# A fourth pair of weight parts, in borrowed homes, for two stretches of an fp32 up projection on one Trainium2 core

## The chip, the core and the metric

The kernel is one program on one core of one Trainium2 chip. The metric is the device time of one execution in microseconds (us). Shorter is better. The engines are named as the profile names them: PE (TensorE, matmuls), PEld (its weight loads), DVE (VectorE), ACT (ScalarE), POOL (GpSimd) and SP (SyncE, which issues most DMAs).

## The reference, cut to what matters

One layer of a decoder trunk, 256 tokens wide 2048, in float32: an RMSNorm, two token mixers, an output projection with a residual, and then the part that the change touches:

```
h = rmsnorm(x, norm_ffn_w)                       # 256 x 2048
gate, up = split(h @ w_up, 2)                    # w_up: 2048 x 11264, so 256 x 5632 each
gate = causal_dwconv(gate, conv_ffn_w) + conv_ffn_b
x = x + (gelu(gate) * up) @ w_down
return rmsnorm(x, norm_final_w)
```

## The kernel before, in words

**High and low parts.** PE multiplies a rounded format (`F32R`) here. To keep float32 accuracy, each operand is cut in two: a high part (the value cast to `F32R`) and a low part (value minus high). A product is then three matmuls: high by high, low by high, high by low. For each weight tile, ACT makes the high part `whi` (the cast, L289), and DVE makes the low part `wlo` (the split, L297: `raw - hi`). A tile is 128 x 2 x 512 (512 KB): 256 rows of the weight matrix by 512 columns.

**Rings.** The raw tile comes by an SP DMA (L209) into a ring of four buffers (tag `raw`). `whi` and `wlo` have rings of three buffers each (`wpool`, L62). `begin(n)` (L277) makes raw loads, casts and splits up to tile number n. `weights()` (L197) is called once for each tile, just ahead of its matmuls, and calls `begin(taken + AHEAD + 1)` with `AHEAD = 2`: when tile number t is used, tiles up to t+2 have been written into the program.

**The up projection.** Its 11264 columns are done in 11 chunks: chunk c covers 512 gate columns and 512 up columns. The 2048 rows are eight pairs of 128, `kp` 0 to 7. A *plain* tile (one column side, one `kp`) takes 12 matmuls (`up_plain`, L1412, through `high_first`, L1368). For chunks in `TWO` (1 to 7 and 9), rows 0 to 1023 are done in another way: in two groups of 512 rows (`ch` 1 first, then 0), a 2 by 2 block product by seven *part* products instead of eight block products (`up_product`, L1377). The blocks of the weights are b11 (first 256 rows of the group, gate), b12 (the same rows, up), b21 and b22 (the next 256 rows). They are loaded whole by SP into the `quad` tiles (`quad_load`, L218), and DVE makes four differences of them in place (`up_sum`, L225, instruction at L230), which with b11, b21 and b22 are the seven factors: T1, 11, T2, 21, T3, 22, T4. Each part tile is cast and split like a raw one, and takes 6 matmuls. Chunks 8 and 10 have one such group, chunk 0 none.

**Order of a step.** `up_steps` (L100 to L127) sets the order of PE by hand (L1446). From chunk 1 to the parts of chunk 7 the same cycle of 22 tiles repeats. I write b for group 1, a for group 0, g4 to g7 and u4 to u7 for the plain tiles of `kp` 4 to 7 on the gate and the up side. The cycle is

```
g4 g5 g6 g7 u4 | T1b u5 11b u6 T1a 11a u7 T2b T2a 21b 21a (turn gate) T3b T3a 22b 22a (turn up) T4b T4a
```

"Step k" below means the parts of chunk k together with the plain tiles of chunk k-1 that come ahead of them. The turns are eight transposes each (L1436) of the finished gate and up results of the chunk before. Beside the splits and the differences, DVE has in each step: two sums that carry a partial result from one PSUM bank to another (L1396 after T2a, which T3b's bank must wait for, since it reads bank `(0, 1)` that T3b goes on to write; and L1410 after T3a, the same with T4b), eight products of the causal convolution (`gate_part`, L1331, two for each of four slices, each pair behind an ACT instruction at L1326), two products of `up_part` (L1344) and the split of the finished result (L1352). These belong to the chunk before and are written into the program one piece at a time behind plain tiles (L1474).

**Who sets the order.** PE's order is that of the program text. The orders of DVE, ACT and of SP's DMA queue are fixed ahead of the run by the framework's planner (L1673, `schedule_with_timeline_sim=True`), which goes by program order as far as it reckons an instruction to be ready. `issue_after` (for example L229) adds a fixed order on one engine: a difference made through `up_sum` outside of `begin` comes behind the last split written so far.

**Homes.** The finished results of chunk c are kept as `hhi{c}` and `hlo{c}` until the down projection (L1345 to L1350). Until then those places of the results 6 to 9 hold `quad` tiles (`UP_HOMES`, L215): for even chunks group 1 lies in `hhi6 hlo6 hhi7 hlo7`, for odd ones in `hhi8 hlo8 hhi9 hlo9`. `hhi5` holds nothing until result 5 is made, behind T4a of step 6. The place `s` (L1279) is used by sums of the activations in chunk 0 and again in chunk 10.

Of the kernel before, what the change touches and what calls it, by code (L numbers as in the profile page):

```python
# [9 lines left out]
F32R = mybir.dt.float32r  # L10
# [25 lines left out]
def kernel(  # L36
# [25 lines left out]
    wpool = ctx.enter_context(tc.tile_pool(name="wpool", bufs=3))  # L62
# [6 lines left out]
    def nm(s):  # L69
        cnt[0] += 1  # L70
        return f"{s}_{cnt[0]}"
# [9 lines left out]
    srcs = []  # L81
# [46 lines left out]
    for step in up_steps:  # L128
        if step[0] == "plain":
            srcs.append(up_w[step[1]][step[2]][step[3]])  # L130
        elif step[0] == "part":
            srcs.append(("up", *step[1:]))
    sums_behind = {}
    for n, src in enumerate(srcs):
        if isinstance(src, tuple):
            what, ch = src[2:]
# [51 lines left out]
    made = []  # L188
    taken = [0]
# [6 lines left out]

    def weights(ahead=AHEAD):  # L197

        begin(taken[0] + ahead + 1)
        taken[0] += 1  # L200
        return made[taken[0] - 1]

# [22 lines left out]
    def up_sum(c, what, ch):  # L225
        b11, b12, b21, b22 = (up_quarters.get((c, ch, i)) for i in range(4))
        for out_, plus_, minus_ in {"T1": [(b12, b12, b11)], "T2": [(b12, b22, b12)],
                                    "T3": [(b11, b12, b11)], "T4": [(b12, b21, b12)]}[what]:
            with tc.issue_after(last_split[0]):  # L229
                nc.vector.tensor_tensor(out_, plus_, minus_, op=ALU.subtract)  # L230
# [6 lines left out]
    def next_quarter():  # L237

        if asked:
            g, i = asked.pop(0)  # L240
            half, chunk, what, home = g // 3, SEVEN[g % 3], ORDER[i], HOMES[g][i]
            r = (fp if home[:2] == "xt" else big).tile([P, 2, 512], F32, tag=home, name=nm("quad"))
            nc.gpsimd.dma_start(r, down[2 * half + int(what[1]) - 1][2 * chunk + int(what[0]) - 1])
            quarters[half, chunk, what] = r
# [9 lines left out]
    def load(n):  # L254
        while len(loads) < min(len(srcs), n):
            m = len(loads)
            for k in range(2) if m < HALVES else (slice(None),):
                load_part(m, k)
# [18 lines left out]
    def begin(n):  # L277
        while len(made) < min(len(srcs), n):
            load(len(made) + 1)
            raw = loads[len(made)]  # L280
            if isinstance(raw, tuple):
                raw, plus, minus = raw
                nc.vector.tensor_tensor(raw, plus, minus, op=ALU.subtract)
            src = srcs[len(made)]
            shape = list(raw.shape)
            keep = kept.get(len(made))
            hi = wpool.tile(shape, F32R, tag="whi", name=nm("whi")) if keep is None else \
                mtile(keep, shape, F32R, nm("khi"))
            nc.scalar.copy(hi, raw)  # L289
            if shape[1] == 8:  # L290
                lo = None
                nc.vector.tensor_tensor(hi[:, :, 32:64], raw[:, :, 0:32], hi[:, :, 0:32].bitcast(F32),
                                        op=ALU.subtract)
            else:
                lo = wpool.tile(shape, F32R, tag="wlo", name=nm("wlo")) if keep is None else \
                    mtile(4 + keep, shape, F32R, nm("klo"))
                last_split[0] = nc.vector.tensor_tensor(lo, raw, hi.bitcast(F32), op=ALU.subtract).ins  # L297
                splits.append(last_split[0])
            made.append((hi, lo))
            for more in sums_behind.get(len(made) - 1, ()):  # L300
                up_sum(*more)
            if isinstance(src, tuple) and src[0] != "up" and src[2] in ("T1", "T3", "T2", "T4"):
                next_quarter()
# [94 lines left out]
    def mtile(i, shape, dt, name):  # L398
        return big.tile(shape, dt, tag=f"m{i}", name=name)
# [228 lines left out]
    for c in range(2):  # L628
        hi, lo = weights()
# [589 lines left out]
    fp = ctx.enter_context(tc.tile_pool(name="ffn", bufs=1))  # L1219
# [119 lines left out]
    def up_part(c, pts):  # L1339

        y = whole[c]
        for f2, pt in enumerate(pts):
            fs = slice(2 * f2, 2 * f2 + 2)
            nc.vector.tensor_tensor(y[:, fs], pt, y[:, fs], op=ALU.mult)  # L1344
        if c < 4:  # L1345
            hh = mtile(c, [P, 4, S], F32R, f"hhi{c}")
            hl = mtile(4 + c, [P, 4, S], F32R, f"hlo{c}")
        else:
            hh = fp.tile([P, 4, S], F32R, tag=f"hhi{c}", name=f"hhi{c}")
            hl = fp.tile([P, 4, S], F32R, tag=f"hlo{c}", name=f"hlo{c}")  # L1350
        nc.scalar.copy(hh, y)
        nc.vector.tensor_tensor(hl, y, hh.bitcast(F32), op=ALU.subtract)  # L1352
        hhi.append(hh)
        hlo.append(hl)
# [22 lines left out]
    def up_product(c, what, ch):  # L1377

        bank = banks_of.setdefault(c, {})
        begins, ends_ = (ch == chunks_of[c][n] for n in (0, -1))  # L1380
        if what in ("11", "21", "T4"):
            j, t = {"11": (0, 0), "21": (1, 0), "T4": (1, 1)}[what]
            high, low = (lambda kk, f=f: f(4 * ch + 2 * j + kk, t) for f in (fh, fl))
        else:
            n = {"T1": 0, "T2": 1, "T3": 2, "22": 3}[what]
            high, low = (lambda kk, s=s: s[:, n, kk * P : (kk + 1) * P] for s in up_ups[ch])
        w = weights()
        if not begins:
            pass
        elif what == "T1":  # L1390
            bank["own"] = pm()[:, 0]
        elif what == "11":
            bank[0, 1] = pg()
        elif what == "21":
            bank[1, 0] = pg()
            last_sum[0] = nc.vector.tensor_tensor(bank[1, 0], bank[0, 1], bank["own"], op=ALU.add).ins  # L1396
        ps = {"T1": "own", "21": (0, 0), "22": (1, 0)}.get(what, (0, 1))
        high_first([(bank[ps], high, low)], w, what in ("T1", "11") and begins)
        if not ends_:
            pass  # L1400
        elif what == "T1":
            own = cpool.tile([P, 512], F32, tag="sqj", name=nm("own"))
            nc.scalar.copy(own, bank["own"])
            bank["own"] = own
        elif what == "11":
            bank[0, 0] = pg()
            last_copy[0] = nc.scalar.copy(bank[0, 0], bank[0, 1]).ins
        elif what == "T3":
            bank[1, 1] = pg()
            last_sum[0] = nc.vector.tensor_tensor(bank[1, 1], bank[0, 1], bank["own"], op=ALU.add).ins  # L1410
# [36 lines left out]
    for i, step in enumerate(up_steps):  # L1447
        if step[0] == "part":
            up_product(*step[1:])
            if step[2] == "T4" and step[3] == chunks_of[step[1]][-1]:  # L1450
                def elementwise(c=step[1] - 1, gates=gates, ups=ups):
                    yield from gate_part(c, gates)
                    up_part(c, ups)
                    yield

                work[:] = [elementwise()]
        elif step[0] == "gate":
            gates = turned_pair(pending[step[1], 0])
        elif step[0] == "up":
            ups = turned_pair(pending[step[1], 1])  # L1460
        elif step[0] == "plain":
            up_plain(*step[1:])
            if step[1:] == (0, 0, 1):
                turned_rows()
            if step[1] == 0 and step[2] == 0 and step[3] in (3, 5):
                with tc.issue_after(last_split[0]):
                    up_ups.append(up_sums(len(up_ups)))
            if step[1] == NUP - 1 and step[2] == 0:
                if step[3] == 5:
                    with tc.issue_after(last_split[0]):  # L1470
                        half_sums(SEVEN[0])
                if 4 <= step[3]:
                    next_quarter()
            if work:  # L1474
                next(work[0], None)
        for n, step in enumerate(up_steps):
            if step[0] == "loads":
                when = (7, 7, 6, 5, 13, 12, 11, 10) if step[1] in TWO else (8, 7, 6, 5)
                for q in sorted(range(len(when)), key=lambda q: -when[q]):
                    if max(n - when[q], 0) == i:  # L1480
                        quad_load(step[1], q)
                if n - 3 == i:
                    up_sum(step[1], "T1", chunks_of[step[1]][0])
    pe_order.close()

# [33 lines left out]
    for hf in range(2):  # L1519
# [11 lines left out]
        for n, step in enumerate(steps[hf]):  # L1531
# [9 lines left out]
            if step[0] == "plain":  # L1541
                kp, c = step[1], step[2] % 2
# [5 lines left out]
            chunk, what = step[1:]  # L1548
# [129 lines left out]
```

## Time and profile before

| | |
|---|---|
| median of 3 runs | 1541.31 us (1539.55 to 1541.64) |
| the profiled execution | 1542.63 us |
| its span in the trace | 1540.8 us |
| granted TensorE clock | 0.999 |
| PE, PEld, DVE, ACT busy | 99%, 82%, 81%, 55% |

The span is what the trace covers of the profiled execution; 1.8 us of its time lie outside. The up projection lies at about 814 to 1300 us of the span. In a timeline row, the columns are start, duration, engine, line, operation, output and inputs, shape and count; the bracket at the end is the engine's idle time just before the row and what ended it. Ends of matmuls are modelled and overlap the next one, so PE is best read from start to start.

### The profile page before, as it was taken

The numbers are of one execution on the slowest core, as the hardware profiler recorded it, in microseconds if no ns is written. First come the engines' busy times: TensorE is split into PE (matmuls) and PEld (weight loads), VectorE is DVE, ScalarE is ACT, GpSimd is POOL, SyncE is SP. The second block draws the span as 40 slices with busy tenths as digits, with TensorE's granted clock in tenths as the row PEclk, the third lists the DMA queues.
The fourth block names the chain that finished last, engine by engine and source line by source line (L and its number), as shares of the span: only waits on it lengthen the run. The fifth ranks groups of instructions, "written<-read, shape, count | busy, mean of one in ns | idle before, by whom it ended". The sixth has DMA issues, their size and how long they took to land.

```text
span 1540.8 us, 20209 instructions
## 1 busy us (share of the span) xinstructions
PE 1526.0 (99%) x7302; PEld 1257.4 (82%) x7302; DVE 1253.4 (81%) x1776; ACT 849.8 (55%) x1063; POOL 70.8 (5%) x90
## 2 busy tenths in 40 slices
PE   9999999999999999999999999999999999999998
PEld 8887888788878888788888888888788888888886
DVE  6788859896589858987667899999999886878885
ACT  7455446454455445454455676666667665555552
POOL 1010002000100000000000000000000000000100
PEclk9999999999999999999999999999999999999999
DMA  8776757776577766776578646666457467556652
GB/s 276 215 221 199 202 163 214 213 214 183 152 245 205 205 169 201 222 200 186 179 250 300 194 163 217 219 205 205 150 155 242 125 216 267 183 193 205 227 189 90
DMA packets 166674, 310.46 MB, mean 201 GB/s; under 512 B 19458, under 2 KB 23330, under 8 KB 166446
## 3 DMA queue, kind: packets, MB, share of 16 engines
q1 hardware_dynamic: 159456, 287.37, 60.0%
q0 software_dynamic: 5184, 18.88, 3.7%
q10 hardware_dynamic: 1934, 2.93, 0.5%
q8 instruction: 57, 0.93, 0.2%
q14 instruction: 43, 0.35, 0.1%
HBM read 301.75 MB, written 7.38 MB: 201 GB/s over the span
## 4 chain that ended last, share of the span: by engine, by line
PE 92%; DVE 4%; issue 2%; DMA 1%; ACT 0%; POOL 0%; POOLq 0%; DVEq 0%; ACTq 0%
PE psg L1374 25%; PE psm L334 15%; PE psm L332 14%; PE psm L333 14%; PE psm L1359 7%; PE psg L1359 7%; DVE wlo L297 3%; PE psm L1374 2%; PE psm L478 1%; PE psg L377 1%; DVE quad L230 1%; PE psm L1436 1%; DMA vrow<-ev 1%; PE psg L868 1%; DMA mv<-vrow 1%
## 5 line engine op out<-in xcount | busy, mean ns | idle before, releaser
L289 ACT CAST whi<-raw 128x1024 fp32r<-128x1024 f32 x428 | 450.0, 1052 | 428.4 <-PE psm L333 280.2
L297 DVE TENSOR_TENSOR wlo<-raw,whi 128x1024 fp32r<-128x1024 f32 x426 | 517.3, 1220 | 151.2 <-ACT whi L289 146.2
L289 ACT CAST whi<-quad 128x1024 fp32r<-128x1024 f32 x168 | 176.1, 1054 | 141.0 <-DVE quad L230 39.4
L297 DVE TENSOR_TENSOR wlo<-quad,whi 128x1024 fp32r<-128x1024 f32 x168 | 202.6, 1219 | 36.2 <-ACT whi L289 35.3
L334 PE MATMUL psm<-wlo,xhl 128*128 128x512 f32 x432 | 169.5, 393 | 1.6 <-DVE wlo L297 1.6
L332 PE MATMUL psm<-whi,xhl 128*128 128x512 f32 x432 | 169.0, 391 | 0.0
L333 PE MATMUL psm<-whi,xhl 128*128 128x512 f32 x432 | 168.6, 390 | 0.0
L1374 PE MATMUL psg<-whi,fhl 128*128 128x512 f32 x504 | 127.1, 389 | 0.0
L1374 PEld LDWEIGHTS psg<-whi,fhl 128*128 128x128 f32 x504 | 94.4, 188 | 19.5
L334 PEld LDWEIGHTS psm<-wlo,xhl 128*128 128x128 f32 x432 | 81.1, 188 | 19.0 <-DVE wlo L297 2.4
L333 PEld LDWEIGHTS psm<-whi,xhl 128*128 128x128 f32 x432 | 81.1, 188 | 16.8
L332 PEld LDWEIGHTS psm<-whi,xhl 128*128 128x128 f32 x432 | 81.1, 188 | 16.6
L230 DVE TENSOR_TENSOR quad<-quad,quad 128x1024 f32<-128x1024 f32 x72 | 87.6, 1217 | 0.0
L1374 PE MATMUL psg<-wlo,fhl 128*128 128x512 f32 x252 | 69.9, 389 | 0.0
L1374 PE MATMUL psg<-whi,ups 128*128 128x512 f32 x216 | 58.9, 394 | 0.0
L1359 PE MATMUL psm<-whi,hhi 128*128 128x512 f32 (+1 forms) x150 | 58.1, 387 | 0.0
L1359 PE MATMUL psm<-whi,hlo 128*128 128x512 f32 (+1 forms) x150 | 57.9, 386 | 0.0
L1359 PE MATMUL psm<-wlo,hhi 128*128 128x512 f32 (+1 forms) x150 | 57.4, 387 | 0.1
L1374 PEld LDWEIGHTS psg<-wlo,fhl 128*128 128x128 f32 x252 | 47.3, 188 | 9.8
L332 PE MATMUL psm<-whi,mhi 128*128 128x512 f32 x128 | 50.8, 397 | 0.0
L1359 PE MATMUL psg<-whi,hhi 128*128 128x512 f32 (+1 forms) x130 | 50.3, 387 | 0.4 <-ACT whi L289 0.4
L1359 PE MATMUL psg<-whi,hlo 128*128 128x512 f32 (+1 forms) x130 | 50.0, 386 | 0.0
(432 smaller groups left out, 2927.3 us busy)
## 6 DMA issues: line engine op xcount, KB each, us to landing
raw<-in_w_in_dram SPq DMA_DIRECT2D x224, 512.0 KB, 4.2
raw<-in_w_up_dram SPq DMA_DIRECT2D x104, 512.0 KB, 4.8
quad<-in_w_up_dram SPq DMA_DIRECT2D x72, 512.0 KB, 4.9
raw<-in_w_down_dram SPq DMA_DIRECT2D x64, 512.0 KB, 4.7
raw<-in_w_out_dram SPq DMA_DIRECT2D x32, 512.0 KB, 4.2
quad<-in_w_down_dram POOLq DMA_DIRECT2D x24, 512.0 KB, 5.5
mv<-vrow SPq DMA_DIRECT2D x12, 512.0 KB, 4.9
taps<-in_conv_qkv_w_dram SPq DMA_DIRECT2D x16, 256.0 KB, 6.8
```

Source lines behind the costliest of these rows:

```text
L230: nc.vector.tensor_tensor(out_, plus_, minus_, op=ALU.subtract)
L289: nc.scalar.copy(hi, raw)
L297: last_split[0] = nc.vector.tensor_tensor(lo, raw, hi.bitcast(F32), op=ALU.subtract).ins
L332: mm(ps[:, t, :], lh(k, t), hi[:, kk, :], start=(k == 0), stop=False)
L333: mm(ps[:, t, :], ll(k, t), hi[:, kk, :], start=False, stop=False)
L334: mm(ps[:, t, :], lh(k, t), lo[:, kk, :], start=False, stop=(k == nk - 1))
L377: nc.tensor.transpose(pt[:, ff, t * P : (t + 1) * P], src[:, t, f * P : (f + 1) * P], ident)
L478: mm(ps_k0[:, t, :], part(k, t), w[:, kk, :], start=(k == 0 and w is hi and part is xh), stop=(k == KD - 1 and w is lo))
L868: mm(pg0, kq[:, h, 0, 0:P], kq[:, h, :, :], start=True, stop=True)
L1359: mm(ps[:, cs], lhs(kk), part_[:, kk, cs], start=(first and kk == 0 and n == 0), stop=(last and kk == 1 and n == 2), skip_group_check=shared)
L1374: mm(ps, lhs(kk), w[n][:, kk], start=(first and n == 0 and kk == 0 and lhs is high), stop=False, skip_group_check=True)
L1436: nc.tensor.transpose(out_[f // 2][:, f % 2, t * P : (t + 1) * P], e[:, t, f * P : (f + 1) * P], ident)
```

## The change

Two stretches of the tile sequence are called deep: from the first plain tile of chunk 1 (g4 behind T4a of step 1) to the tile ahead of T3b of step 6, and from g4 behind T4a of step 6 to the tile ahead of T3 of step 8. In them, every fourth tile has its high part in a home of a result that isn't there yet (`hhi5` in the first stretch, `hhi7` in the second) and its low part in `s`; the three others go through the rings of three as before, so that together they work as a ring of four. `weights()` then calls `begin` with one tile more, so casts and splits are written one tile further ahead of PE. The first difference (T1) of steps 2 to 8 is written one step sooner to match. The raw ring stays at four, and the homes of the `quad` tiles stay as they are. No instruction of the computation is added or taken away.

```diff
+    part_at = {tuple(src[1:]): n for n, src in enumerate(srcs) if isinstance(src, tuple)}
+
+    def first_part(c, what="T1"):
+        return min(n for (c_, what_, _), n in part_at.items() if c_ == c and (what_ == what or what is None))
+
+    DEEP = ((first_part(1, "T4") + 2, first_part(6, "T3"), "hhi5"),
+            (1 + max(n for (c_, what_, _), n in part_at.items() if (c_, what_) == (6, "T4")), first_part(8, "T3"), "hhi7"))
+
+    def deep(n):
+        return next(((n - a, tag) for a, b, tag in DEEP if a <= n < b), None)
...
     def weights(ahead=AHEAD):
 
-        begin(taken[0] + ahead + 1)
+        begin(taken[0] + ahead + (2 if deep(taken[0] + ahead + 1) else 1))
...
             keep = kept.get(len(made))
-            hi = wpool.tile(shape, F32R, tag="whi", name=nm("whi")) if keep is None else \
-                mtile(keep, shape, F32R, nm("khi"))
+            fourth = deep(len(made))
+            if fourth and fourth[0] % 4 == 3:
+                hi = fp.tile(shape, F32R, tag=fourth[1], name=nm("whi"))
+            else:
+                fourth = None
+                hi = wpool.tile(shape, F32R, tag="whi", name=nm("whi")) if keep is None else \
+                    mtile(keep, shape, F32R, nm("khi"))
             nc.scalar.copy(hi, raw)
...
-                lo = wpool.tile(shape, F32R, tag="wlo", name=nm("wlo")) if keep is None else \
-                    mtile(4 + keep, shape, F32R, nm("klo"))
+                if fourth:
+                    lo = fp.tile(shape, F32R, tag="s", name=nm("wlo"))
+                else:
+                    lo = wpool.tile(shape, F32R, tag="wlo", name=nm("wlo")) if keep is None else \
+                        mtile(4 + keep, shape, F32R, nm("klo"))
...
-                if n - 3 == i:
+                if n - (4 if 2 <= step[1] <= 8 else 3) == i:
                     up_sum(step[1], "T1", chunks_of[step[1]][0])
```

## The prediction

> **What bounds the kernel now.** I read the page first, then PE's waits, then the up projection in stretches of one step, then the rows around each wait.
>
> ```profile
> span 1540.8 us, 20209 instructions
> ...
> PE 1526.0 (99%) x7302; PEld 1257.4 (82%) x7302; DVE 1253.4 (81%) x1776; ACT 849.8 (55%) x1063; POOL 70.8 (5%) x90
> ```
> ```profile
> PE psg L1374 <- DVE wlo L297: 4.0, 7, 0.6
> ```
> ```profile
> 838.00:882.00 44.00, 44.00 (x204) 36.63 (x203) 39.18 (x40) 27.90 (x31) 0.00 (x0) 1.00 0.57 186
> 882.00:925.50 43.50, 42.91 (x198) 35.31 (x197) 40.34 (x42) 31.09 (x35) 0.00 (x0) 1.00 0.51 167
> 925.50:969.00 43.50, 42.89 (x198) 35.31 (x197) 41.18 (x44) 29.35 (x34) 0.00 (x0) 1.00 0.57 193
> ```
>
> PE is the bound nearly everywhere, so only its waits can be won. In the up projection (L1374) the trace has seven, all for a low part from DVE. The stretches (span, then PE, PEld, DVE busy) show PE without a gap in the step at 838 us and with one in the two that follow; DVE is then busy 41.18 of 43.50 us. The granted clock is 1.00 in all of them. The 4.0 us are idle behind a modelled end, so I measure from start to start, in steps 2, 6 and 7:
>
> ```profile
> 920.88 1.07 PE L1374 MATMUL psg<-whi,ups 128*128 128x512 f32 x4
> 921.79 0.62 PE L1374 MATMUL psg<-wlo,ups 128*128 128x512 f32 x2
> 922.25 1.09 PE L1374 MATMUL psg<-whi,ups 128*128 128x512 f32 x4
> 923.93 0.73 PE L1374 MATMUL psg<-wlo,ups 128*128 128x512 f32 x2 [0.59 <-DVE wlo L297]
> ...
> 1094.95 1.08 PE L1374 MATMUL psg<-whi,ups 128*128 128x512 f32 x4
> 1096.37 0.73 PE L1374 MATMUL psg<-wlo,ups 128*128 128x512 f32 x2 [0.34 <-DVE wlo L297]
> 1096.94 1.09 PE L1374 MATMUL psg<-whi,ups 128*128 128x512 f32 x4
> 1098.64 0.73 PE L1374 MATMUL psg<-wlo,ups 128*128 128x512 f32 x2 [0.61 <-DVE wlo L297]
> ...
> 1140.46 1.08 PE L1374 MATMUL psg<-whi,ups 128*128 128x512 f32 x4
> 1142.14 0.73 PE L1374 MATMUL psg<-wlo,ups 128*128 128x512 f32 x2 [0.60 <-DVE wlo L297]
> ```
>
> Four matmuls on `whi` take 0.91 us when nothing is late (920.88 to 921.79). At the last part ahead of the second turn (22a) they take 1.68 (922.25 to 923.93): 0.77 lost. Step 7 loses the same, steps 3 to 5 between 0.75 and 0.81 at the same place, and step 6 twice: 1.42 - 0.91 = 0.51 and 1.70 - 0.91 = 0.79. In all 0.77 x 5 (steps 2 to 5 and 7, rounded) + 1.30 = **5.15 us**, 0.33% of the time. That is the most the change can win. PE's own pace is 43.50 - 0.77 = 42.73 us a step.
>
> Why is 22a late? The answer differs between step 2 and the later ones.
>
> ```profile
> 898.60 1.22 DVE L297 TENSOR_TENSOR wlo<-quad,whi 128x1024 fp32r<-128x1024 f32 x1 [0.91 <-ACT whi L289]
> 914.11 1.23 DVE L297 TENSOR_TENSOR wlo<-quad,whi 128x1024 fp32r<-128x1024 f32 x1 [0.61 <-ACT whi L289]
> ```
> ```profile
> 901.64 1.05 ACT L289 CAST whi<-quad 128x1024 fp32r<-128x1024 f32 x1 [1.26 <-PE psg L1374]
> 911.11 1.06 ACT L289 CAST whi<-quad 128x1024 fp32r<-128x1024 f32 x1 [0.66 <-PE psg L1374]
> ```
>
> In step 2, DVE stands still again and again (0.91 and 0.61 are the largest gaps) until a cast is done, and the casts wait until PE gives back a `whi`: the ring of three is short, and the time that DVE loses there is missing at 22a. In step 3 the picture is another:
>
> ```profile
> 924.40 0.47 DVE L1331 SCALAR_TENSOR_TENSOR y<-psm,cfw,y 128x255 f32<-128x255 f32 x1
> 924.79 2.35 DVE L297 TENSOR_TENSOR wlo<-quad,whi 128x1024 fp32r<-128x1024 f32 x2
> 927.06 0.47 DVE L1331 SCALAR_TENSOR_TENSOR y<-psm,cfw,y 128x254 f32<-128x254 f32 x1
> 927.45 2.34 DVE L297 TENSOR_TENSOR wlo<-raw,whi 128x1024 fp32r<-128x1024 f32 x2
> ...
> 935.27 1.23 DVE L297 TENSOR_TENSOR wlo<-raw,whi 128x1024 fp32r<-128x1024 f32 x1 [1.51 <-ACT whi L289]
> ...
> 938.83 1.22 DVE L297 TENSOR_TENSOR wlo<-quad,whi 128x1024 fp32r<-128x1024 f32 x1 [0.28 <-ACT whi L289]
> ...
> 942.83 1.22 DVE L1352 TENSOR_TENSOR hlo<-y,hhi 128x1024 fp32r<-128x1024 f32 x1 [0.45 <-ACT hhi L1351]
> ```
> ```profile
> 934.19 1.05 ACT L289 CAST whi<-raw 128x1024 fp32r<-128x1024 f32 x1 [1.88 <-DMA raw<-in_w_up_dram]
> ```
> ```profile
> 928.69 4.55 SPq L209 DMA_DIRECT2D raw<-in_w_up_dram  x4
> ```
>
> Here DVE's whole idle time is 1.51 + 0.28 + 0.45 = 2.24 us, and none of it waits for PE. The 1.51 is u4: its load is issued at 928.69, when the split of g4 (927.45, of a row of two) has given back the first of the four raw buffers; it has landed at 934.19, 5.5 us later. From 938.83 on DVE doesn't stop but for the 0.45. So DVE runs a loop of its own, split of g4, load of u4, 33 us of splits and sums, next split of g4: 41.18 + 2.24 = 43.4 us, against 42.73 for PE. PE is carried along by it and shows the difference as a wait at 22a.
>
> **The change part by part.** No instruction is added. The fourth tiles are cast and split by the same ACT and DVE instructions into other places; I cost that at nothing (the places are 128 x 1024 like the rings'). The bound on the other side is a `whi` or `wlo` row that differs by where it lies; the single splits above take 1.22 or 1.23, so 26 + 8 fourth tiles by 0.01 = 0.3 us on DVE, a gain or a loss, hidden by the DVE idle above. The homes are free: `hhi5` and `s` have no reader left in the first stretch, `hhi7` none in the second. So no wait is added there.
>
> *Step 2.* With one tile more ahead, a cast waits for the tile before, that is one part's time on PE less: 922.25 - 920.88 = 1.37 us. The gaps of DVE there are all below that, so they close as far as is needed; 22a comes 0.77 earlier, and up to 1.37 - 0.77 = 0.6 us of lead remains. Gain 0.77.
>
> *Steps 3 to 5 and 7.* The fourth buffer doesn't bring u4's raw tile sooner by itself. What can is DVE's order. Before, the first two convolution products (L1331) run ahead of the splits of T4b and of g4, in places where the planner had no split ready; from row to row each costs 0.39 (924.40 to 924.79, 927.06 to 927.45). With splits written one tile ahead and buffers for them, they have reason to go behind g4. Then g4's split ends 0.78 sooner, u4 is loaded and lands 0.78 sooner, and the 0.78 of products fall into the gap of 1.51. The loop becomes 43.4 - 0.78 = 42.6 us, just under PE's 42.73, and the lead of step 2 covers small misses. The bounds: with the order unchanged the loop stays at 43.4 and loses 0.7 of lead a step (gain 0); with all 1.51 filled it is 41.9 (gain limited by PE). I take the value in between, which lets PE run at its own pace: gain 4 x 0.77 for 3, 4, 5 and 7 = 3.1.
>
> *Step 6.* The stretch ends at T3b of this step, and before, u4's gap was longer here:
>
> ```profile
> 1066.51 1.23 DVE L297 TENSOR_TENSOR wlo<-raw,whi 128x1024 fp32r<-128x1024 f32 x1 [2.22 <-ACT whi L289]
> ```
>
> 0.71 more than in step 3, so the loop would be 0.6 us longer than PE's pace, and the three buffers at its end give no cover. Between 0 and 1.30 gained; I take 0.6.
>
> *T1 a step sooner.* Its `issue_after` ties it to the last split written, which is u4's in both versions (before: two tiles ahead of g6; after: three ahead of g5). So it stays behind u4 on DVE and can't fill the gap. Nothing.
>
> *SP's queue.* The raw loads of g4 to g7 are written one tile sooner, past the `quad` loads of the next chunk in some places. In the trace the last of them before step 3 is issued long ahead of need:
>
> ```profile
> 908.06 0.37 SPq L209 DMA_DIRECT2D raw<-in_w_up_dram  x1
> ```
>
> That is 19 us ahead of g4's split (927.45), so the shift costs nothing. The bound: were the `quad` loads held behind u4's raw load, they would come as late as that load itself, and with them T1a's difference; I give that no more than the scatter.
>
> Sum: 0.77 + 3.1 + 0.6 = 4.5 us. The profiled execution took 1542.63 us (span 1540.8 and 1.8 outside), so it would take 1538.1; it stood 1.3 above the median of 1541.31, from which I forecast **1536.8 us**.
>
> The Trainium skill, page "Perfetto Trace Analysis", section "Optimization Strategy", says that a gap that repeats on the engine that should be saturated can mean that too few buffers are there for the next tile. The rows of step 2 agree (casts that wait 1.26 and 0.66 for PE); those of step 3 do not, where DVE waits for a load. By the rule alone all seven waits would go, and the sum would be 5.15.
>
> **The rivals.**
>
> *The loads keep the loop.* The planner leaves the order of L1331 and g4 as it is. Then step 2 gains 0.77, step 3 lives on its lead of 0.6, and the waits are back in full from step 4 on: 1.4 us, with up to 1 more from step 6: 1539.9. For it: DVE's idle of step 3 waits for no buffer that the change adds. Against it: those two L1331 ran ahead of splits that had been written before them. That the change hardly moves anything because the planner casts no sooner than before is the same outcome, at 1541.3.
>
> *The sum between banks comes late (slower).* T3b may start only when L1396 has read bank (0, 1):
>
> ```profile
> 915.25 1.22 DVE L230 TENSOR_TENSOR quad<-quad,quad 128x1024 f32<-128x1024 f32 x1
> 916.39 0.69 DVE L1396 TENSOR_TENSOR psg<-psg,own 128x512 f32<-128x512 f32 x1
> ```
> ```profile
> 918.06 1.17 PE L1374 MATMUL psg<-whi,ups 128*128 128x512 f32 x4
> ```
>
> L1396 ends at 917.08, 0.98 before T3b starts. After the change the splits of T3b and T3a and the T4b difference stand ahead of it in the program, at 1.14 us each (915.25 to 916.39). One of them ahead costs 0.16, which is nothing; from two on it costs more than the wait that it replaces (2.28 - 0.98 = 1.30 against 0.77); with all three 3.42 - 0.98 = 2.44, less 0.77 won at 22a, is 1.67 a step. In steps 2 to 5 and 7: 8.3 us, so 1549.6. Against it: before, the planner put L1396 ahead of T3b's split, which was written sooner too, and T3a's cast follows its own sum, so its split can hardly be ready. The Trainium skill, page "TensorE: Matmul & The Clock Gate", section "Architectural detail", says that DVE's queue is strictly first in, first out, so an order once planned isn't mended at run time; the wait at 22a behind sums shows no overtaking either.
>
> **How the numbers follow.** About 0.2%, 3.1 us, is what a measurement can tell from no change. The forecast case (3.1 to 5.15 gained) has 0.57, the loads keeping the loop or nothing moving (0 to 3) 0.30, the late bank sum 0.13. So faster 0.57, same 0.30, slower 0.13. The low end is all 5.15 gained and 1 us of scatter (the three runs spread over 2.1): 1535.2. The high end takes in the case without gain: 1541.6. What is left out is the slow rival and little else. The forecast case alone is 1535.2 to 1538.2.
>
> **What would show it.** Right: the PE waits for L297 at L1374 fall from seven to one or two, the steps stand 42.7 us apart, u4's gap on DVE is about 0.7 with L1331 rows behind g4's split, and casts in step 2 no longer wait for PE. Wrong: waits at 22a from step 4 on with u4's gap still near 1.5 (first rival), or PE waiting for DVE L1396 at T3b (second). A gain from anywhere but these seven places would mean that I misread the chain.

## The result: 22.7 us slower

| | before | changed |
|---|---|---|
| median | 1541.18 us | 1563.92 us (1562.26 to 1564.46, 4 runs) |
| ratio to before | | 1.0149, 95% interval 1.0135 to 1.0164 |
| profiled execution, its span | 1542.63, 1540.8 us | 1564.46, 1562.7 us |
| granted clock | 0.999 | 0.993 |

The line numbers are those of the changed kernel here: the matmuls of the up projection are L1393 (were L1374), splits L316 (L297), convolution products L1350 (L1331), their ACT instruction L1345 (L1326), the bank sums L1415 and L1429 (L1396 and L1410). PE's waits in the changed kernel (total, count, longest):

```profile
PE psm L1393 <- DVE y L1350: 16.9, 5, 3.9
...
PE psg L1393 <- DVE wlo L316: 0.8, 1, 0.8
```

Six of the seven waits for a low part are gone, as forecast. In their place stand five for something that the prediction never named: a matmul into a `psm` bank that waits for a convolution product. PE's rows in step 3:

```profile
922.16 1.07 PE L1393 MATMUL psg<-whi,ups 128*128 128x512 f32 x4
923.07 0.63 PE L1393 MATMUL psg<-wlo,ups 128*128 128x512 f32 x2
...
939.83 1.07 PE L1393 MATMUL psg<-wlo,fhl2a 128*128 128x512 f32 x4
944.50 1.76 PE L1393 MATMUL psm<-whi,ups 128*128 128x512 f32 x4 [3.60 <-DVE y L1350]
946.06 1.05 PE L1393 MATMUL psm<-wlo,ups 128*128 128x512 f32 x2
946.91 2.62 PE L1393 MATMUL psg<-whi,fhl2b 128*128 128x512 f32 x8
949.37 1.09 PE L1393 MATMUL psg<-wlo,fhl2b 128*128 128x512 f32 x4
950.30 1.07 PE L1393 MATMUL psg<-whi,fhl1a 128*128 128x512 f32 x4
```

22a (the first two rows) runs at 0.91 us, without a wait. T1b, the `psm` row, was due 0.91 us behind 939.83, at 940.74, and starts at 944.50: 3.76 late. The same wait is 4.04, 4.06 and 3.79 in steps 4, 5 and 6, and about 2.0 before T1 of step 8: 17.65 us in all. It doesn't end there. From T1b to 11b (950.30) the 18 matmuls of T1b and u5 should take 0.91 + 0.45 + 1.81 + 0.91 = 4.08 us, and take 5.80. The stretches of the changed kernel (span, PE, PEld, DVE, ACT, POOL busy, granted clock, DMA) show why:

```profile
940.00:944.00 4.00, 0.90 (x4) 0.40 (x3) 4.00 (x6) 1.08 (x2) 0.00 (x0) 1.00 0.79 278
944.00:947.00 3.00, 2.50 (x7) 2.01 (x8) 1.64 (x3) 1.76 (x2) 0.00 (x0) 0.64 0.53 167
947.00:950.00 3.00, 3.00 (x12) 2.41 (x11) 2.36 (x2) 1.72 (x3) 0.00 (x0) 0.79 0.00 0
950.00:960.00 10.00, 10.00 (x45) 8.27 (x45) 8.11 (x7) 6.59 (x8) 0.00 (x0) 1.00 0.19 54
```

Behind the idle time, the granted clock is 0.64 and then 0.79, and 1.00 again from 950 us on. That costs 1.72 us here and, reckoned in the same way, 1.59, 2.96 and 1.70 in steps 4 to 6, 8.0 together; behind the shorter wait of step 8, matmuls run at the usual pace. Sum: 17.65 + 8.0 lost, 5.15 won, about 1.0 of it still there in step 6: 21.5, against 21.8 between the two profiled executions.

**Whom T1b waits for.** T1's own sum is kept in a bank of `pm()` (L1410 in the changed kernel's `up_product`), a pool of two. The turned gate and the turned up results hold both. T1b gets the gate's, when the last convolution product has read it. In the profile of before, that product ends at 938.54, 3.2 us ahead of T1b's start:

```profile
937.55 0.99 DVE L1331 SCALAR_TENSOR_TENSOR y<-psm,cfw,y 128x255 f32<-128x255 f32 x2
```
```profile
941.71 1.07 PE L1374 MATMUL psm<-whi,ups 128*128 128x512 f32 x4
```

DVE's rows of the changed kernel at the same place:

```profile
930.00 0.48 DVE L1350 SCALAR_TENSOR_TENSOR y<-psm,cfw,y 128x255 f32<-128x255 f32 x1
932.33 1.23 DVE L316 TENSOR_TENSOR wlo<-raw,whi 128x1024 fp32r<-128x1024 f32 x1 [1.85 <-ACT whi L305]
933.47 1.22 DVE L241 TENSOR_TENSOR quad<-quad,quad 128x1024 f32<-128x1024 f32 x1
934.61 0.48 DVE L1350 SCALAR_TENSOR_TENSOR y<-psm,cfw,y 128x254 f32<-128x254 f32 x1
935.88 1.23 DVE L316 TENSOR_TENSOR wlo<-quad,whi 128x1024 fp32r<-128x1024 f32 x1 [0.80 <-ACT whi L305]
937.03 0.48 DVE L1350 SCALAR_TENSOR_TENSOR y<-psm,cfw,y 128x255 f32<-128x255 f32 x1
937.42 1.22 DVE L316 TENSOR_TENSOR wlo<-raw,whi 128x1024 fp32r<-128x1024 f32 x1
938.55 0.48 DVE L1350 SCALAR_TENSOR_TENSOR y<-psm,cfw,y 128x254 f32<-128x254 f32 x1
938.95 1.22 DVE L316 TENSOR_TENSOR wlo<-quad,whi 128x1024 fp32r<-128x1024 f32 x1
940.08 1.22 DVE L241 TENSOR_TENSOR quad<-quad,quad 128x1024 f32<-128x1024 f32 x1
941.21 0.48 DVE L1350 SCALAR_TENSOR_TENSOR y<-psm,cfw,y 128x255 f32<-128x255 f32 x1
941.60 1.22 DVE L316 TENSOR_TENSOR wlo<-raw,whi 128x1024 fp32r<-128x1024 f32 x1
942.74 1.22 DVE L241 TENSOR_TENSOR quad<-quad,quad 128x1024 f32<-128x1024 f32 x1
943.87 0.48 DVE L1350 SCALAR_TENSOR_TENSOR y<-psm,cfw,y 128x254 f32<-128x254 f32 x1
```

Between any two products stand one to three splits or differences. Over the eight products these are 13, where before there were 8; each takes about 1.13 us (from 937.42 to 938.55, for example). The last product ends at 944.35, and T1b starts at 944.50. DVE is no busier in all than before (1253.9 against 1253.4 us); it does the urgent work last. It even stands idle for 1.85 us ahead of u4's split (932.33), while the second product of slice 2 (934.61), whose first ended at 930.48, comes two places later in the order fixed ahead. The length of the chain decides: in steps 3 to 6 it takes 20.8 to 21.1 us and T1b waits about 4, in step 8 it takes 19.0 and T1b waits 2.0, and in step 7 it takes 16.0 and T1b doesn't wait. ACT's part of the chain in the changed kernel:

```profile
927.85 0.57 ACT L1345 ACTIVATE y<-psm,vec,cfw 128x256 f32<-128x256 f32 x1
...
935.76 0.56 ACT L1345 ACTIVATE y<-psm,vec,cfw 128x256 f32<-128x256 f32 x1
...
939.46 0.57 ACT L1345 ACTIVATE y<-psm,vec,cfw 128x256 f32<-128x256 f32 x1
```

Each of these, slices 2, 3 and 4, starts only when both products of the slice before are done (the second ones end at 927.82, 935.09 and 939.03). The kernel before has the same tie, and there a row names it:

```profile
931.75 0.57 ACT L1326 ACTIVATE y<-psm,vec,cfw 128x256 f32<-128x256 f32 x1 [0.57 <-DVE y L1331]
```

So the chain goes to and fro between two engines, and at each return the planner has found DVE something else to do.

### The profile page after: what moved, and what is told of

Its sections match the earlier page's. It is cut to its first block, busy times and chain, and to the rows that moved or that the text cites. A ratio compares the mean times of both kernels' runs of the same rounds, so it can differ in the third digit from the quotient of the medians.

```text
span 1562.7 us, 20199 instructions
## 1 busy us (share of the span) xinstructions
PE 1533.5 (98%) x7302; PEld 1263.7 (81%) x7302; DVE 1253.9 (80%) x1776; ACT 850.8 (54%) x1063; POOL 71.3 (5%) x90
## 4 chain that ended last, share of the span: by engine, by line
PE 93%; DVE 3%; DMA 2%; issue 1%; ACT 1%; POOL 0%; POOLq 0%; DVEq 0%; ACTq 0%
PE psg L1393 27%; PE psm L353 14%; PE psm L351 14%; PE psm L352 14%; PE psm L1378 7%; PE psg L1378 6%; PE psm L1393 2%; PE psm L497 1%; PE psm L1455 1%; DVE wlo L316 1%; PE psg L396 1%; DMA vrow<-ev 1%; DVE quad L241 1%; PE psg L887 1%; DMA mv<-vrow 1%
## 5 line engine op out<-in xcount | busy, mean ns | idle before, releaser
L316 DVE TENSOR_TENSOR wlo<-raw,whi 128x1024 fp32r<-128x1024 f32 x426 | 517.8, 1222 | 152.7 <-ACT whi L305 147.7
L316 DVE TENSOR_TENSOR wlo<-quad,whi 128x1024 fp32r<-128x1024 f32 x168 | 204.3, 1223 | 49.7 <-ACT whi L305 48.3
L1393 PE MATMUL psg<-whi,fhl 128*128 128x512 f32 x504 | 127.1, 389 | 0.0
L1393 PEld LDWEIGHTS psg<-whi,fhl 128*128 128x128 f32 x504 | 94.5, 188 | 19.5
L1393 PE MATMUL psg<-wlo,fhl 128*128 128x512 f32 x252 | 69.9, 389 | 0.0
L1393 PE MATMUL psg<-whi,ups 128*128 128x512 f32 x216 | 58.8, 394 | 0.0
L1393 PEld LDWEIGHTS psg<-wlo,fhl 128*128 128x128 f32 x252 | 47.3, 188 | 9.8
```

The source lines that it names most:

```text
L1393: mm(ps, lhs(kk), w[n][:, kk], start=(first and n == 0 and kk == 0 and lhs is high), stop=False, skip_group_check=True)
```

## The experiments

Theory A: the wait is for the bank, because the planner spreads the convolution products among splits that the fourth buffers have made ready. Rivals: B, the text that is written one tile further ahead pushes the products back; C, the borrowed places or late loads are to blame. Beside these stands the question what share the clock has.

**e2_buffers_only.** Does the order of the text matter?

```diff
-        begin(taken[0] + ahead + (2 if deep(taken[0] + ahead + 1) else 1))
+        begin(taken[0] + ahead + 1)
...
-                if n - (4 if 2 <= step[1] <= 8 else 3) == i:
+                if n - 3 == i:
```

> The changed kernel with only its fourth buffers: begin is called with one tile less, as before the change, and T1 is written as late as before. Theory A (the fourth buffer makes splits ready that the planner puts between the convolution products, so the PSUM bank that T1b needs is read too long): the text order does not matter, 1563.9 within 1.5, and again five PE waits for a convolution product, four of about 3.6 to 3.9 us. Theory B (splits written one tile further ahead push the convolution products back): the waits go, 1537 to 1541.

Measured 1562.17 us (2 runs; ratio to before 1.0142, 1.0123 to 1.0160), with the five waits:

```profile
PE psm L1393 <- DVE y L1350: 16.7, 5, 4.0
```

The planner gives every engine the same order of work as in the changed kernel. Theory B is out: with the buffers there, `weights()` looking one tile further changes nothing, and without it the buffers alone bring the whole loss.

**e3_keep_warm.** What does the clock cost?

```diff
         elif what == "T1":
+            if 3 <= c <= 6:
+                bank[0, 1] = pg()
+                for _ in range(17):
+                    mm(bank[0, 1].rearrange("p (a s) -> p a s", a=2), fh(0, 0), both(fhl, 0), start=True, stop=True,
+                       skip_group_check=True)
             bank["own"] = pm()[:, 0]
         elif what == "11":
-            bank[0, 1] = pg()
+            if (0, 1) not in bank:
+                bank[0, 1] = pg()
```

> The changed kernel with 17 extra matmuls of 128x512 (about 3.86 us, results not used) ahead of T1b in steps 3 to 6, in the bank that 11b starts afresh later. They fill PE's wait but shorten nothing that it waits for. Theory A with the clock (part of the loss is PE's slower pace behind the idle time): T1b starts at the same time, its matmuls and u5's run at the usual pace, 8.0 us less in all, 1556. If the slow pace were a wait for data instead: 1564, or some more where the extra matmuls overrun the wait.

Measured 1555.64 us (2 runs; 1.0099, 1.0081 to 1.0118): 8.3 less than the changed kernel. T1b of step 3 starts when it did, now behind useless work instead of idle time, and runs at the usual pace:

```profile
944.37 1.17 PE L1393 MATMUL psm<-whi,ups 128*128 128x512 f32 x4 [0.21 <-DVE y L1350]
```

So 8 of the 22.7 us are not the wait but what follows it. The Trainium skill, page "TensorE: Matmul & The Clock Gate", section "Part 1: The HAM clock gate", says that about 3.4 us without work halve PE's clock until it has been busy as long again. The runs agree: idle times of 3.6 to 3.9 us are followed by slow matmuls, the one of 1.84 is not, and the usual pace is back some 3 to 6 us later.

**e8_bank_copied and e10_all_copied.** Free the bank early and leave the rest.

```diff
             gates = turned_pair(pending[step[1], 0])
+            if 2 <= step[1] <= 4 or step[1] == 1:
+                moved = fp.tile([P, 2, 2, S], F32, tag="hlo5", name=nm("moved"))
+                for f2 in range(2):
+                    nc.scalar.copy(moved[:, f2], gates[f2])
+                gates = [moved[:, f2] for f2 in range(2)]
```

e10 does so up to chunk 6 (`if 1 <= step[1] <= 6`, with `hlo6` for the sixth).

> The changed kernel, but for the chunks 1 to 4 ACT copies the turned gate out of its PSUM bank at once (two copies of 128x512, about 0.59 us each, into the place hlo5), and the convolution products read the copy. Theory A: T1b of steps 3 to 6 no longer waits, whatever DVE's order is; the waits of 15.7 us and 8.0 us of slow matmuls go and only the 2.0 us at T1 of step 8 stays: 1564 - 23.7 = 1540, a little more if the extra ACT work is felt. Theory C (borrowed places or late loads are to blame): 1562 to 1566.

> The changed kernel with the copy of the turned gate for the chunks 1 to 6 (in hlo5, the sixth in hlo6), so that T1 of step 8 doesn't wait for the bank either. Theory A: the last wait for a convolution product (1.95 us before T1 of step 8, 2.1 from start to start) goes and nothing else changes: 1538.75 - 2.1 = 1536.6, which would be the forecast of the change itself. If the copies only shift the wait: 1538 to 1540.

Measured 1538.75 us for e8 (10 runs; 0.9984, 0.9975 to 0.9993) and 1537.57 for e10 (11 runs; 0.9978, 0.9969 to 0.9987). In e8 one such wait is left, the one before T1 of step 8:

```profile
PE psm L1393 <- DVE y L1350: 2.0, 1, 2.0
```

In e10 there is none, and of the waits for a low part in the up projection two are left:

```profile
PE psg L1393 <- DVE wlo L316: 1.2, 2, 1.0
```

Both of these fall in step 6, where the first deep stretch ends. That is theory A, and C is out: the fourth parts lie where they lay. e10 came out between its two expected outcomes, and its gain on e8 is not clear of the scatter (the intervals overlap). The copies do more than free the bank, though: in the planner's order the two products of a slice now follow each other and the chain takes 7.8 us (step 3), so DVE's order isn't that of the changed kernel. The two runs don't tell a bank that is free early from a chain that is short.

**e7_conv_first.** Put the order right by force.

```diff
-                last_split[0] = nc.vector.tensor_tensor(lo, raw, hi.bitcast(F32), op=ALU.subtract).ins
+                n = len(made)
+                held = any(0 <= n - first_part(c) < 3 for c in range(2, 9))
+                with tc.issue_after(last_conv[0]) if held else ExitStack():
+                    last_split[0] = nc.vector.tensor_tensor(lo, raw, hi.bitcast(F32), op=ALU.subtract).ins
...
```

(`last_conv` holds the latest convolution product; the lines that set it are left out here.)

> The changed kernel, but the splits of the first three tiles from T1 on (T1b, u5, 11b) are put behind the last convolution product on DVE, for steps 2 to 8. The fourth buffers stay. Theory A: all five waits go, the seven waits at 22a stay away, PE runs at its own pace: 1537, the time that was forecast. Theory C: 1560 or more. If the order costs elsewhere what it wins (splits of T1b to 11b late): 1541 to 1548.

Measured 1547.09 us (5 runs; 1.0041, 1.0028 to 1.0053). No matmul waits for a convolution product any more, but:

```profile
PE psg L1398 <- DVE wlo L320: 4.8, 6, 1.6
...
PE psg L1398 <- DVE psg L1420: 1.3, 2, 0.8
```

That is the third outcome. PE now waits for low parts of other tiles: T3a and T4b of step 3, T1a and T2a of step 5, 22a and T4a of step 6. In two steps it waits for the sum between banks (L1420 here), which is the prediction's slow rival in small. The wait for the bank goes when the products go first, and an order forced at three places is not the cure.

**e5_acts_first and e13_acts_first_timed.** Take the to and fro out of the chain: all four ACT instructions are written first, then the products (one kernel under two names).

```diff
             with tc.issue_after(last_copy[0]) if c < NUP - 1 else ExitStack():
                 nc.scalar.activation(y[:, f, :], pt, AF.Identity, scale=cfw[:, 2 * KF + r : 2 * KF + r + 1],
                                      bias=vec[:, V_CB + r : V_CB + r + 1])
+        for f in range(4):
+            r = 4 * c + f
+            pt = pts[f // 2][:, f % 2, :]
             with tc.issue_after(last_sum[0]) if c < NUP - 1 else ExitStack():
```

> The changed kernel with the four ACT instructions of the convolution written ahead of the eight DVE products. Theory A (the products' places in DVE's order decide): 1562 to 1564 with the same five waits. If the to and fro between ACT and DVE is what stretches the chain: the waits shrink by some 0.6 us for each of three ACT legs, 1555 or less.

Measured 1536.13 us in the one run. That is on the side of the second outcome, but 27.8 us less than the changed kernel where three legs of 0.6 us in five steps would give 9. I had taken DVE's order as given; but the planner makes another one as soon as a slice's products needn't wait for ACT. ACT's and DVE's rows of this kernel, step 3:

```profile
916.64 1.93 ACT L1345 ACTIVATE y<-psm,vec,cfw 128x256 f32<-128x256 f32 x4 [0.24 <-PE psm L1458]
```
```profile
924.58 0.87 DVE L1353 SCALAR_TENSOR_TENSOR y<-psm,cfw,y 128x254 f32<-128x254 f32 x2
925.36 2.35 DVE L316 TENSOR_TENSOR wlo<-raw,whi 128x1024 fp32r<-128x1024 f32 x2
927.63 0.87 DVE L1353 SCALAR_TENSOR_TENSOR y<-psm,cfw,y 128x254 f32<-128x254 f32 x2
928.41 1.22 DVE L316 TENSOR_TENSOR wlo<-raw,whi 128x1024 fp32r<-128x1024 f32 x1
929.54 0.87 DVE L1353 SCALAR_TENSOR_TENSOR y<-psm,cfw,y 128x254 f32<-128x254 f32 x2
930.77 1.22 DVE L316 TENSOR_TENSOR wlo<-raw,whi 128x1024 fp32r<-128x1024 f32 x1 [0.36 <-ACT whi L305]
```

The four run one after the other at 916.64, and the products go in pairs, though splits still stand between the pairs. The chain takes 12.7 us in this step. Timed:

> The same kernel as e5_acts_first (the changed one with the four ACT instructions written ahead of the eight products), timed. Theory A as it now stands (ACT's instruction for one slice stands behind DVE's products of the slice before; each round trip gives the planner room to put the splits that the fourth buffers made ready in between; so the bank is held too long): the waits at T1b and at 22a are both gone but for one of 0.4 us, 1536.1 within 1 us. If the single run was luck: 1538 to 1541.

Measured 1538.20 us (10 runs; 0.9978, 0.9969 to 0.9988), above the 1537.1 that I gave as the upper end: the single run was a lucky one. It is clearly below before all the same. In steps 3 to 6 the chain takes 12.7 to 14.9 us, and T1b doesn't wait, with the products still read from the bank. One wait of 0.4 us for a low part is left in the up projection.

**e11_before_copied and e12_before_acts_first.** Are the fourth buffers worth anything, or do the two cures do it alone? The kernel before, with the edit of e10 and with that of e13.

> The kernel before (rings of three, nothing further ahead) with the same copies for the chunks 1 to 6. It tells what the fourth buffers themselves are worth once the bank is free early. If the fourth buffers win the waits at 22a, as forecast: 1541 here, with seven waits at 22a, against 1536.6 with them. If the copies alone loosen DVE's order and win them: 1536 to 1538, and the fourth buffers are worth nothing.

> The kernel before (rings of three) with the ACT instructions written ahead of the products. If the fourth buffers are what wins the waits at 22a: those waits stay, 1540 to 1542, and the fourth buffers are worth 4 to 5 us on top of this edit. If the new order alone loosens DVE's loop: 1536 to 1538, and the fourth buffers are worth nothing.

Measured 1546.82 us (5 runs; 1.0037, 1.0023 to 1.0050) and 1548.16 (5 runs; 1.0042, 1.0029 to 1.0056). Both lose, which I had not expected. In e11 and in e12 the waits for a low part grew:

```profile
PE psg L1374 <- DVE wlo L297: 8.4, 12, 0.8
```
```profile
PE psg L1377 <- DVE wlo L297: 9.6, 6, 1.6
```

With rings of three, products that are ready sooner are put ahead of splits that PE needs. In step 2 of e11 four products stand ahead of T4b's split (before, one), and PE waits for that split, on top of the wait at 22a:

```profile
922.68 1.66 DVE L1331 SCALAR_TENSOR_TENSOR y<-moved,cfw,y 128x255 f32<-128x255 f32 x4
924.25 2.35 DVE L297 TENSOR_TENSOR wlo<-quad,whi 128x1024 fp32r<-128x1024 f32 x2
```
```profile
925.52 0.73 PE L1374 MATMUL psg<-wlo,fhl1b 128*128 128x512 f32 x2 [0.79 <-DVE wlo L297]
```

In e12 a bank sum and one product (0.99 us together, from 922.60 to 923.59) go ahead of 22a's split, and the wait at 22a grows from 0.60 to 1.60 us. Both repeat in each of the steps 2 to 7. With the fourth buffers the same two edits gain: 1546.82 becomes 1537.57, 1548.16 becomes 1538.20. The buffers are worth 9 to 10 us once the bank is out of the way, of which 5.6 and 6.8 make good what the cure alone loses; neither half is worth anything alone.

**e9_before_late_conv.** The kernel before, its last two products held behind u5's split.

```diff
-            with tc.issue_after(last_sum[0]) if c < NUP - 1 else ExitStack():
+            if f == 3 and 1 <= c <= 4:
+                yield
+                yield
+                yield
+            with tc.issue_after(last_split[0] if f == 3 and 1 <= c <= 4 else last_sum[0]) if c < NUP - 1 else ExitStack():
```

> The kernel before, without any fourth buffer, but in the steps 3 to 6 the last two convolution products are put behind the split of u5 on DVE, so that they end at about 943.1 instead of 938.5 us in step 3, where T1b is due at 940.7 plus the wait of its step. Theory A (a late reader of the bank is enough): PE waits for L1331-like rows of 1.4 to 2.2 us at T1b in four steps, in place of the wait at 22a, at full clock behind it: 1544 to 1547. Theory C (the borrowed places are needed for the loss): 1541.

Measured 1542.99 us (8 runs; 1.0014, 1.0004 to 1.0024): inconclusive as a time, since it lies between the two outcomes. The delay used up the slack and not more; one step alone has a wait, of 0.9 us:

```profile
PE psm L1378 <- DVE y L1335: 0.9, 1, 0.9
```

Its rows say more than its time. In each of the four steps T1b starts 0.15 or 0.16 us behind the last product, as it does in the changed kernel; it is on time with that in steps 4 and 5, 0.1 us late in step 3 and 1.1 in step 6, counted from start to start. So the tie to the bank is there without any fourth buffer, but a loss of the expected size was not brought about. Step 4 shows how close it is, as that product's row ends at 982.64:

```profile
981.65 0.99 DVE L1335 SCALAR_TENSOR_TENSOR y<-psm,cfw,y 128x255 f32<-128x255 f32 x2
```
```profile
982.81 1.15 PE L1378 MATMUL psm<-whi,ups 128*128 128x512 f32 x4
```

## Why the prediction was wrong

- **The step that failed** is in "Steps 3 to 5 and 7": convolution products that go behind splits were costed as a gain of 0.78 us a step, with nothing on the other side. I asked what such a move frees, and never who waits for the products. "So no wait is added there" holds for the homes, which cost nothing in e8, e10 and e13, but the only bank for which I asked about an added wait was T3b's. The measured term is a wait of 3.8 to 4.1 us at T1b in each of the steps 3 to 6, 2.0 in step 8, and 8.0 of slow matmuls behind them. The answer was in the profile of before: T1b's bank, with a slack of 3.2 us. The chain of eight products, from 924.40 to 938.54 before, runs from 923.54 to 944.35 after: 6.7 us longer (five more splits and differences at 1.13 us, and about 1.1 us more of idle time), which is twice the slack. Step 7, counted with steps 3 to 5, is the one that kept its slack.
- **No rival named it.** The slow rival had the right kind (a bank that DVE still has to read) at the wrong place: L1415 was done in time in the changed kernel and came late only in e7.
- **The 5.15 us to be won** were right in place: six of seven waits went. That most of it can be had shows in e10 and e13: by their ratios 3.4 us below before, with an interval from about 2 to 4.8 that includes the 4.5 that I took.
- **Step 2**, ring of three too short: right in its result, as 22a no longer waits. The sign that I named for it didn't come: casts of step 2 still wait for PE, up to 1.21 us (at 905.64) against 1.26 before.
- **Steps 3 to 5**, u4's gap to shrink to 0.7: wrong, it grew to 1.85 in step 3 of the changed kernel. The load itself did come sooner, and by more than the 0.78 that I reckoned: g4's split starts 2.4 us sooner than before (925.07 for 927.45) and u4's cast 2.9 (931.25 for 934.19). But in DVE's order u4's split comes sooner still, ahead of products that could have run. In e5 the gap is 0.36.
- **Text order.** I derived the new order of DVE from splits "written one tile ahead and buffers for them". e2 shows that the first half does nothing and the buffers alone do it. That they do it by making splits ready sooner fits the rows, but is argued from them.
- **The clock.** I took PE's pace as fixed at 1.00. A third of the loss, 8.3 of 22.7 us, is a granted clock that falls behind idle times of 3.6 us and more, and not behind those of 1.84 and less.

Left open: why the planner, given ready splits, prefers them to the second product of a slice (product, split, product) when the products read PSUM, and not when they read a copy (e10). That wasn't tried apart.

## What to carry to other kernels

A deeper buffer changes more than the wait that it is meant for. Here a planner fills an engine with what it takes to be ready; more buffers made more splits ready, and these went ahead of a chain whose links come back from another engine one by one. Before adding a buffer, list who holds what until the displaced work is done (here a PSUM bank), and compare the slack with the number of displaced steps times their duration (here five more steps of 1.13 us, against 3.2 us of slack). Make the chain short first (all links of one engine together), then deepen the buffer: here each alone was slower than before, both together were 0.2% faster.

## What the runs showed of the hardware

In the changed kernel and in e2, idle times of PE of 3.5 to 4.0 us were each followed by matmuls at about half pace, up to 0.43 us for 128x512 instead of 0.227 (u5 of step 5 in the changed kernel: eight in 3.41 us), until some 3 to 6 us later; each cost 1.6 to 3.0 us on top of the wait. The wait of 1.84 us at step 8 had no such sequel. So the four waits of 3.8 to 4.1 us in the changed kernel are priced at 5.5 to 7.0 us each, 5.9 on average.
